# One core, a hybrid decoder block: the RWKV chunk chain with both heads in one matmul, the first two projection tiles in token halves, and the second up product added into the first one's copy

## The chip, the cores and the metric

The kernel is one program on one NeuronCore of a Trainium2 chip. The metric is the device time of one execution in microseconds (us); lower is better. Three runs of the kernel before took 2916.89 to 2919.65 us, with a median of 2918.94 us. TensorE (PE) multiplies; VectorE (DVE), ScalarE (ACT) and GpSimd (POOL) work on tiles; the queue of SyncE (SP) and the queues of ACT and POOL issue DMA transfers.

## The reference, cut to what matters

The block takes x of 512 tokens by 2048 channels in float32. It normalises x, projects it to 9,152 columns of several kinds, runs RWKV-7 time mixing (16 heads of 64) and sliding-window attention side by side, merges both with gates, projects back, and adds a gated ConvFFN of width 5632.

```python
h = rms_norm(x, norm1_g[l])
z = h @ w_in[l]                       # every projection; token shift on the RWKV part
def step(state, inp):                 # RWKV, for each head, token after token
    r_t, k_t, v_t, w_t, ka_t, kb_t = inp
    sa = jnp.einsum('bhvk,bhk->bhv', state, ka_t)
    state = (state * w_t[:, :, None, :] + sa[..., None] * kb_t[:, :, None, :]
             + v_t[..., None] * k_t[:, :, None, :])
    y = jnp.einsum('bhvk,bhk->bhv', state, r_t)
    return state, y
x = x + (g_rw * p_rw + g_att * p_att) @ w_out[l]
u = h2 @ w_up                         # h2 = rms_norm(x, norm2_g); then a causal conv of
val, gate = jnp.split(c, 2, axis=-1)  # width 3 over tokens gives c
x = x + (silu(gate) * val) @ w_down
```

## The kernel before, in words

**Precision.** A float32 operand of a large product is split into a high part (`whi`, `xhi`: an ACT copy to the type float32r) and the rest (`wlo`, `xlo`: a DVE subtraction), and three float32r matmuls replace one exact one: hi by hi, hi by lo, lo by hi. Small products stay plain float32; the trace shows each of those as two PE instructions.

**Order.** A planner orders the instructions of each engine by its own cost model and then every engine runs its list strictly in that order. `pin` (`tc.keep_in_program_order`) puts an instruction behind the one written just before it for the same engine, so the planner may not move it ahead; an instruction without `pin` may be moved ahead of earlier ones.

**Start (L291 to L310).** Four x tiles of 128 tokens are loaded and squared for the norm. In two halves of 256 tokens they are scaled (L297) and transposed on PE block by block (L304), and each block is evicted to `xhi` by ACT (L306) and to `xlo` by DVE (L307). Only when all 16 blocks of both halves exist does the first projection tile start.

**Projection tiles (`ztile`, `project`, `load_w`).** A tile is 128 columns of `w_in` for all 512 tokens: 16 blocks of 128 input channels by three matmuls of 512 columns (L259 to L261) into one PSUM bank. `load_w` (L241 to L245) loads four blocks of weights by SP into one of four `raw` buffers and splits them. After each third `load_w` it sends one job ahead for later stages (`sums_along`): SP copies half a megabyte in DRAM (L228) and POOL adds another half to it by DMA (L229). The first tiles are a key tile and a value tile of the attention (`c_ka`, `c_va`).

**RWKV (L464 to L800).** Heads go in eight pairs, one head in partitions 0 to 63 and one in 64 to 127. `early(p)` makes a pair's inputs with three projection tiles, `late(p)` builds and inverts the within-chunk matrices and then runs the chain over eight chunks of 64 tokens; `final(p)` and three gate tiles follow. While the chain of one pair waits, the planner fills PE with the next pair's projections and the gate tiles. In the chain each head has matmuls of its own, with 64 columns of weights and 64 moving columns, into its half of the partitions: `psG` (L744), `psS` (L755), and for the output `y` the products with `MM` (L765) and `BAR` (L767). `psU` (L748) already takes both heads at once.

**Up stage (L1049 to L1290).** One Strassen-like scheme gives for each block f of 128 columns seven products P1, P2, P7, P6, P5, Q4, P3 of 24 matmuls of 256 columns each (L1095). The first four blocks run P1, then P2, then P7 for all four while the right-hand factors t3, t1, t2, b22, t4 are still being made by DVE and split (`split_q`: ACT copy L1042, DVE subtraction L1043). For these four, P1 sits in one half of a PSUM bank (X) and P2 in the other half (Z). P1 is copied to `t1` (L1104); P2 stays in Z until the tiles `u` exist, and only then does `out("P2")` write `u = t1 + Z` (L1115). P6, P5 and P3 are accumulated onto P1 in X, and between them ACT copies X out to `u` (L1111). `run(i)` prepares step i + 2 (`prep`: the sum of two weight blocks L1071, then `whi` L1077 and `wlo` L1078), issues the matmuls of step i and then takes its result out.

Of the kernel before, what the change touches and what calls it, by code (L numbers as in the profile page):

```python
# [135 lines left out]
def block_kernel(ctx: ExitStack, tc: tile.TileContext, d: Dims, a: dict, out: bass.AP):  # L136
# [94 lines left out]
    wp = {"n": 0, "step": 3}  # L231
# [5 lines left out]
    def load_w(src):  # L237
# [4 lines left out]
        hi = wp["hl"].tile([P, 512], F32R, name="whi", tag="whi")[:, :n].rearrange("p (k c) -> p k c", c=ncol)  # L242
        lo = wp["hl"].tile([P, 512], F32R, name="wlo", tag="wlo")[:, :n].rearrange("p (k c) -> p k c", c=ncol)
        act.activation(hi, raw, AF.Copy)  # L244
        dve.tensor_tensor(lo, raw, hi.bitcast(F32), op=ALU.subtract)  # L245
        wp["n"] += 1
        if wp["n"] % wp["step"] == 0:
            sums_along()()
        return hi, lo

    def project(acc, src, xhi, xlo, pre=()):
        nk = src.shape[1]
        for k0 in range(0, nk, 4):
            n = min(4, nk - k0)
            whi, wlo = pre[k0 // 4] if k0 // 4 < len(pre) else load_w(src[:, k0 : k0 + n])
            for j in range(n):
                k = k0 + j
                first, last = k == 0, k == nk - 1
                pe.matmul(acc, whi[:, j], xhi[:, k], start=first, stop=False)  # L259
                pe.matmul(acc, whi[:, j], xlo[:, k], start=False, stop=False)  # L260
                pe.matmul(acc, wlo[:, j], xhi[:, k], start=False, stop=last)  # L261
# [3 lines left out]
    sync.dma_start(sinkb, a["attn_sinks"].rearrange("(o h) -> o h", o=1).to_broadcast([P, d.HQ]))  # L265
    sync.dma_start(cst, a["cst"][:, P:])
# [17 lines left out]
    if True:  # L284
# [3 lines left out]
        with tc.tile_pool(name="x0_ps", bufs=6, space=PSUM) as ps0:  # L288
            ssum = p0.tile([P, NT], F32, name="ssum")
            HT = NT // 2  # L290
            for h in range(2):  # L291
                for t in range(h * HT, (h + 1) * HT):
                    sq = p0.tile([P, d.D], F32, name="sqx", tag="sqx", bufs=1)
                    act.activation(sq, xt[t], AF.Square, accum_out=ssum[:, t : t + 1])
                r = rsqrt_small(p0, ssum[:, h * HT : (h + 1) * HT], 1.0 / d.D, RMS_EPS)
                for t in range(HT):
                    dve.tensor_scalar(xt[h * HT + t], xt[h * HT + t], r[:, t : t + 1], None, op0=ALU.mult)  # L297
            first = {d.c_ka: [load_w(zt[d.c_ka][:, k0 : k0 + 4]) for k0 in range(0, min(NK, 12), 4)]}
            for h in range(2):
                hs = slice(h * HT * P, (h + 1) * HT * P)  # L300
                for k in range(NK):
                    ps = ps0.tile([P, HT * P], F32, name="ps_x", tag="x")
                    for t in range(HT):
                        pe.transpose(ps[:, t * P : (t + 1) * P], xt[h * HT + t][:, k * P : (k + 1) * P], ident)  # L304
                    g = col("n1g", k)
                    act.activation(xhi[:, k, hs], ps, AF.Identity, scale=g)  # L306
                    dve.scalar_tensor_tensor(xlo[:, k, hs], ps, g, xhi[:, k, hs].bitcast(F32), op0=ALU.mult, op1=ALU.subtract)  # L307
        xin.close()
        act.activation(bor, K["bo"], AF.Copy)
        act.activation(cenr, K["cen"], AF.Copy)  # L310

        accp = pa.enter_context(tc.tile_pool(name="accA", bufs=3, space=PSUM, side="right", reuse_waits="tile"))

        def ztile(c0):
            acc = accp.tile([P, S], F32, name="acc", tag="acc")
            project(acc, zt[c0], xhi, xlo, first.pop(c0, ()))
            return acc
# [156 lines left out]
        with ExitStack() as pr:  # L474
# [141 lines left out]
            def late(p, st):  # L616
# [123 lines left out]

                for n in range(NCH):
                    ps = chn.tile([P, C], F32, name="psG", tag="chn")
                    for h, (lo, hi) in enumerate(HV):
                        pe.matmul(ps[lo:hi], AB[:, n, h], SV[:, n, h], start=True, stop=True)  # L744
                    G = wk.tile([P, C], F32, name="G", tag="G", bufs=2)
                    dve.tensor_copy(G, ps)
                    ps = chn.tile([P, C], F32, name="psU", tag="chn")
# [5 lines left out]
                    ps = chn.tile([P, C], F32, name="psS", tag="chn")  # L753
                    for h, (lo, hi) in enumerate(HV):
                        pe.matmul(ps[lo:hi], KK[:, n, h], UV[:, n, h], start=True, stop=True)  # L755
                    for h, (lo, hi) in enumerate(HV):
                        dve.scalar_tensor_tensor(SV[lo:hi, n + 1, h], SV[lo:hi, n, h], ee[lo:hi, n : n + 1], ps[lo:hi],
                                                 op0=ALU.mult, op1=ALU.add)


                ps = bulk()
                for n in range(NCH):
                    for h, (lo, hi) in enumerate(HV):
                        dst = r3(ps)[lo:hi, n]
                        pe.matmul(dst, UV[:, n, h], MM[:, n, h], start=True, stop=n == 0)  # L765
                        if n:
                            pe.matmul(dst, SV[:, n, h], BAR[:, n, h, 1], start=False, stop=True)  # L767
                yhl = wk.tile([P, 2, S], F32R, name="yhl", tag="rhl")
                split(yhl[:, 0], yhl[:, 1], ps)
# [270 lines left out]
    def split_q(n, q):  # L1040
        hi, lo = (halves(x) for x in bq[n])
        act.activation(hi, q, AF.Copy)  # L1042
        dve.tensor_tensor(lo, q, hi.bitcast(F32), op=ALU.subtract)  # L1043
# [7 lines left out]
    class Block:  # L1051
# [46 lines left out]
        def out(self, n):  # L1098
# [3 lines left out]
            if n == "P1" and self.f < NPRE:  # L1102
                self.t1 = up.tile([P, TH], F32, name="t1", tag="t1", bufs=NPRE)
                pin(act.activation(self.t1, X, AF.Copy))  # L1104
                return

# [7 lines left out]
            else:  # L1114
                pin(dve.tensor_tensor(u, self.t1 if n == "P2" and self.f < NPRE else u, ps, op=ALU.add))  # L1115
# [78 lines left out]
    def run(i):  # L1194
# [3 lines left out]
        if n != "P2" or f >= NPRE:  # L1198
            B[f].out(n)
# [9 lines left out]
    with tc.tile_pool(name="sqp", bufs=1, side="right", reuse_waits="tile") as sqp:  # L1209
# [3 lines left out]
        for i in range(len(PRODUCTS)):  # L1213
# [6 lines left out]
            for c in range(NB["o"]):  # L1220
                steps_of("o", i, acc[nm], c, hp)
                if last and c == NB["o"] - 4:
                    transposed(tps, 0, q11)
                    split_q("b11", q11)
                if last and c == NB["o"] - 3:
                    transposed(tps, 1, q21)
                    split_q("b21", q21)
# [27 lines left out]
    dve.tensor_tensor(q12, q22, q12, op=ALU.subtract)  # L1255
    split_q("t3", q12)
    tcx.close()
    x1q.close()
    run(5)
# [5 lines left out]
    dve.scalar_tensor_tensor(q11, q11, -1.0, q22, op0=ALU.mult, op1=ALU.subtract)  # L1265
# [5 lines left out]
    dve.scalar_tensor_tensor(q21, q11, -1.0, q21, op0=ALU.mult, op1=ALU.subtract)  # L1271
# [10 lines left out]
    for f in range(2):  # L1282
        B[f].out("P2")
    for i in range(3 * NPRE, len(steps)):
        run(i)
        if steps[i] in ((2, "P6"), (2, "Q4")):
            B[2 + (steps[i][1] == "Q4")].out("P2")
# [106 lines left out]
```

## Time and profile before

| | us |
|---|---|
| median of three runs | 2918.94 |
| the profiled execution, its own time | 2915.49 |
| its span, first to last instruction | 2913.7 |
| PE busy | 2868.1 |
| DVE busy | 1970.2 |
| ACT busy | 1333.6 |
| PE busy in the first 35 us | 14.48 |
| PE busy from 1576 to 1683 us (107 us, the opening of the up stage) | 94.54 |
| PE busy from 340 to 1180 us (840 us, the RWKV pairs) | 837.27 |

How to read it: times count from the first instruction of the profiled execution. A row of a timeline gives start, duration, engine, line, operation, output and inputs, shape, number of instructions merged, and in brackets how long the engine had been idle and what ended that. Matmuls overlap in the array, so durations of neighbours overlap too; what one costs is the distance from its start to the next start. `PEclk` is the share of the TensorE clock that was granted.

### The profile page before, as it was taken

How to read it: one execution, taken by the hardware profiler on the slowest of the kernel's cores; microseconds unless marked ns; L12 is line 12 of the kernel's file. 1: busy time of each engine (PE TensorE's matmuls, PEld its weight loads, DVE VectorE, ACT ScalarE, POOL GpSimd, SP SyncE). 2: the span in 40 equal slices, each digit the busy share in tenths (PEclk: the TensorE clock that was granted, in tenths of full speed). 3: DMA queues.
4: the chain of work that ended last, by engine and by line, in shares of the span. 5: the costliest groups of instructions: out<-in, count | busy, mean ns of one | idle time of the engine just before them, and what ended most of it. 6: DMA issues, size and time to landing. Idle time of an engine off the chain costs nothing.

```text
span 2913.7 us, 46929 instructions
## 1 busy us (share of the span) xinstructions
PE 2868.1 (98%) x18014; PEld 2441.3 (84%) x18014; DVE 1970.2 (68%) x3383; ACT 1333.6 (46%) x2251; POOL 219.3 (8%) x286
## 2 busy tenths in 40 slices
PE   7999999999999999999999899999999999999999
PEld 5777777777777777788888899999999999888887
DVE  4577666667767766354567777787777777665565
ACT  4345435435435434322356455545555455544444
POOL 0001000000000000111000010111111100000000
PEclk9999999999999999999999999999999999999999
DMA  7856756656656655878877788988889888877775
GB/s 210 217 146 166 184 142 168 156 145 163 159 149 149 167 148 139 266 222 239 293 251 226 208 227 231 242 233 231 221 235 238 237 227 234 312 242 240 259 255 188
DMA packets 225137, 609.29 MB, mean 209 GB/s; under 512 B 24768, under 2 KB 44944, under 8 KB 223888
## 3 DMA queue, kind: packets, MB, share of 16 engines
q1 hardware_dynamic: 157504, 434.84, 45.9%
q0 software_dynamic: 36064, 132.14, 23.9%
q10 hardware_dynamic: 31344, 39.31, 4.0%
q8 instruction: 141, 2.31, 0.3%
q14 instruction: 84, 0.69, 0.1%
HBM read 556.54 MB, written 174.43 MB: 251 GB/s over the span
## 4 chain that ended last, share of the span: by engine, by line
PE 94%; DVE 2%; ACT 1%; DMA 1%; issue 0%; SPq 0%; DVEq 0%; ACTq 0%
PE X L1095 17%; PE acc L259 11%; PE X L962 11%; PE acc L261 11%; PE acc L260 11%; PE Y L1095 9%; PE Y L962 8%; PE Z L1095 4%; PE bulk L737 1%; PE bulk L690 1%; PE psG L744 1%; PE bulk L646 1%; PE psS L755 1%; PE mi L464 1%; PE scp L431 1%; PE bulk L554 1%
## 5 line engine op out<-in xcount | busy, mean ns | idle before, releaser
L259 PE MATMUL acc<-xhi,whi 128*128 128x512 f32 x1152 | 473.1, 411 | 5.0 <-ACT whi L244 3.1
L261 PE MATMUL acc<-xhi,wlo 128*128 128x512 f32 x1152 | 469.2, 408 | 0.0
L260 PE MATMUL acc<-xlo,whi 128*128 128x512 f32 x1152 | 467.1, 405 | 0.0
L244 ACT ACTIVATE whi<-raw 128x512 fp32r<-128x512 f32 x352 | 220.3, 630 | 492.8 <-PE acc L260 376.6
L955 DVE TENSOR_TENSOR wlo<-raw,whi 128x1024 fp32r<-128x1024 f32 x210 | 257.0, 1224 | 204.9 <-ACT whi L954 203.4
L245 DVE TENSOR_TENSOR wlo<-raw,whi 128x512 fp32r<-128x512 f32 x352 | 240.2, 689 | 207.3 <-ACT whi L244 195.4
L954 ACT ACTIVATE whi<-raw 128x1024 fp32r<-128x1024 f32 x210 | 222.8, 1061 | 287.9 <-PE X L962 147.1
L1095 PE MATMUL X<-b,whi 128*128 128x256 f32 x1472 | 270.2, 284 | 2.2 <-DVE u L1115 0.9
L1095 PE MATMUL X<-t,whi 128*128 128x256 f32 x1408 | 260.2, 285 | 8.7 <-DVE u L1115 8.3
L1078 DVE TENSOR_TENSOR wlo<-raw,whi 128x1024 fp32r<-128x1024 f32 x176 | 215.0, 1222 | 77.4 <-ACT whi L1077 77.2
L259 PEld LDWEIGHTS acc<-xhi,whi 128*128 128x128 f32 x1152 | 217.5, 189 | 52.8 <-ACT whi L244 4.4
L261 PEld LDWEIGHTS acc<-xhi,wlo 128*128 128x128 f32 x1152 | 217.3, 189 | 48.2 <-issue 2.2
L1095 PE MATMUL Y<-t,whi 128*128 128x256 f32 x1408 | 257.5, 283 | 0.0
L260 PEld LDWEIGHTS acc<-xlo,whi 128*128 128x128 f32 x1152 | 217.7, 189 | 44.9 <-issue 3.3
L1077 ACT ACTIVATE whi<-a 128x1024 fp32r<-128x1024 f32 x132 | 139.4, 1056 | 213.8 <-DVE a L1071 211.2
L1095 PEld LDWEIGHTS X<-b,whi 128*128 128x128 f32 x1472 | 230.3, 193 | 3.0 <-issue 2.3
L1095 PEld LDWEIGHTS X<-t,whi 128*128 128x128 f32 x1408 | 222.0, 194 | 9.3 <-DVE u L1115 5.7
L1095 PEld LDWEIGHTS Y<-t,whi 128*128 128x128 f32 x1408 | 220.1, 192 | 0.0
L1095 PE MATMUL X<-b,wlo 128*128 128x256 f32 x736 | 208.9, 284 | 2.1 <-DVE wlo L1078 2.1
L1078 DVE TENSOR_TENSOR wlo<-a,whi 128x1024 fp32r<-128x1024 f32 x132 | 161.7, 1225 | 67.7 <-ACT whi L1077 67.0
L1095 PE MATMUL X<-t,wlo 128*128 128x256 f32 x704 | 200.5, 285 | 0.0
L1095 PE MATMUL Y<-t,wlo 128*128 128x256 f32 x704 | 199.3, 283 | 0.0
(345 smaller groups left out, 5877.7 us busy)
## 6 DMA issues: line engine op xcount, KB each, us to landing
raw<-in_w_up_dram SPq DMA_DIRECT2D x180, 512.0 KB
raw<-in_w_z_dram SPq DMA_DIRECT2D x288, 256.0 KB
s_dn<-in_w_dn_dram POOLq DMA_DIRECT2D x88, 512.0 KB, 6.7
raw<-in_w_up_dram POOLq DMA_DIRECT2D x88, 512.0 KB, 8.1
raw<-s_dn SPq DMA_DIRECT2D x88, 512.0 KB
raw<-in_w_dn_dram SPq DMA_DIRECT2D x66, 512.0 KB
a<-in_w_up_dram SPq DMA_DIRECT2D x48, 512.0 KB
s_dn<-in_w_dn_dram SPq DMA_DIRECT2D x44, 512.0 KB
```

Of the source, the lines that this page charges most:

```text
L244: act.activation(hi, raw, AF.Copy)
L245: dve.tensor_tensor(lo, raw, hi.bitcast(F32), op=ALU.subtract)
L259: pe.matmul(acc, whi[:, j], xhi[:, k], start=first, stop=False)
L260: pe.matmul(acc, whi[:, j], xlo[:, k], start=False, stop=False)
L261: pe.matmul(acc, wlo[:, j], xhi[:, k], start=False, stop=last)
L431: pe.matmul(scp[e][:, j, k0:], qn[j][hs, ts], kd[g][hs, n * P - BLK + k0 : (n + 1) * P], start=True, stop=True)
L954: act.activation(whi, wr, AF.Copy)
L955: dve.tensor_tensor(wlo, wr, whi.bitcast(F32), op=ALU.subtract)
L962: pe.matmul(dst, l[:, q, ts], r[:, es], start=fst and j == 0, stop=lst and j == 2, skip_group_check=True)
L1077: pin(act.activation(hi, t, AF.Copy))
L1078: pin(dve.tensor_tensor(lo, t, hi.bitcast(F32), op=ALU.subtract))
L1095: pin(pe.matmul(ps, l[:, k], r[:, k], start=start and k + i == 0, stop=last and i == 2, skip_group_check=True))
```

## The change

**Chain.** `psG` and `psS` become one matmul each for both heads (128 columns of weights, 128 moving columns); the blocks that mix two heads are computed too and never read. `G` is taken out by ACT for one head and DVE for the other. `y` is made by one `MM` and one `BAR` matmul for a chunk into two PSUM banks, one for four chunks, and split in eight quarter pieces in place of one whole.

```diff
                 for n in range(NCH):
-                    ps = chn.tile([P, C], F32, name="psG", tag="chn")
-                    for h, (lo, hi) in enumerate(HV):
-                        pe.matmul(ps[lo:hi], AB[:, n, h], SV[:, n, h], start=True, stop=True)
+                    ps = chn.tile([P, 2, C], F32, name="psG", tag="chn")
+                    pe.matmul(heads2(ps), heads2(AB[:, n]), heads2(SV[:, n]), start=True, stop=True)
                     G = wk.tile([P, C], F32, name="G", tag="G", bufs=2)
-                    dve.tensor_copy(G, ps)
+                    act.copy(G[0:C], ps[0:C, 0])
+                    dve.tensor_copy(G[C:P], ps[C:P, 1])
...
+                    pe.matmul(heads2(ps), heads2(KK[:, n]), heads2(UV[:, n]), start=True, stop=True)
                     for h, (lo, hi) in enumerate(HV):
-                        pe.matmul(ps[lo:hi], KK[:, n, h], UV[:, n, h], start=True, stop=True)
+                        dve.scalar_tensor_tensor(SV[lo:hi, n + 1, h], SV[lo:hi, n, h], ee[lo:hi, n : n + 1], ps[lo:hi, h],
+                                                 op0=ALU.mult, op1=ALU.add)
...
+                for g in range(2):
+                    ps = bulk().rearrange("p (n h c) -> p n h c", h=2, c=C)
+                    for j in range(HN):
+                        n = g * HN + j
+                        pe.matmul(heads2(ps[:, j]), heads2(UV[:, n]), heads2(MM[:, n]), start=True, stop=n == 0)
+                        if n:
+                            pe.matmul(ps[:, j], heads2(SV[:, n]), BAR[:, n, :, 1], start=False, stop=True)
                     for h, (lo, hi) in enumerate(HV):
-                        dst = r3(ps)[lo:hi, n]
-                        pe.matmul(dst, UV[:, n, h], MM[:, n, h], start=True, stop=n == 0)
-                        if n:
-                            pe.matmul(dst, SV[:, n, h], BAR[:, n, h, 1], start=False, stop=True)
-                split(yhl[:, 0], yhl[:, 1], ps)
+                        own = [r3(yhl[lo:hi, e])[:, g * HN : (g + 1) * HN] for e in range(2)]
+                        split(own[0], own[1], ps[lo:hi, :, h])
```

**Start.** The first two tiles (`heads`) run in halves of 256 tokens, with `half_mm` issuing three matmuls of 256 columns for a block. The first tile's first half follows the transposes of the first token half; the second tile's first half is laid between the transposes of the second token half; the two second halves come last. All of this is pinned. The weights of both tiles have eight pairs of buffers of their own beside the x tiles. The PSUM ring of the transposes goes from six to five, the two small constant loads go behind the first weights on SP, and the two DRAM jobs that these loads used to send are sent after the 31st and the 34th `load_w`.

```diff
-    wp = {"n": 0, "step": 3}
+    wp = {"n": 2 * NK // 4, "step": 3}
...
-        if wp["n"] % wp["step"] == 0:
+        if wp["n"] % wp["step"] == 0 or wp["n"] in (31, 34):
...
+            r = scales(0)
+            for t in range(HT):
+                scaled(0, t, r, dve)
+            ws = [[], []]
+            for k in range(NK):
+                columns(0, k)
+                if k == NK // 2 - 1:
+                    r = scales(1)
+                if k >= NK // 2 and k % 2:
+                    weights(0, 2 * (k - NK // 2 - 1))
+            for t in range(HT):
+                scaled(1, t, r, act if t else dve)
+            sync.dma_start(cst, a["cst"][:, P:])
...
+            for k in range(NK):
+                half_mm(0, 0, k)
+            for k in range(NK):
+                if k % 4 == 0:
+                    weights(1, k)
+                columns(1, k)
+                half_mm(1, 0, k)
+            for i in range(2):
                 for k in range(NK):
...
+                    half_mm(i, 1, k)
```

**Up stage.** For the first four blocks P2 is added to `t1` by DVE right after its matmuls; `placed` later copies `t1` to `u` on ACT. The splits and subtractions that make t3, t1, t2, b22 and t4 are now pinned where they are written, and the split of t3 moves ahead by one step.

```diff
+            if n == "P2" and self.f < NPRE:
+                pin(dve.tensor_tensor(self.t1, self.t1, Z, op=ALU.add))
+                return
...
+        def placed(self):
+
+            pin(act.activation(us[self.f % 2][:, 0, 2 : 2 + TH], self.t1, AF.Copy))
...
-    dve.tensor_tensor(q11, q11, q12, op=ALU.subtract)
+    pin(dve.tensor_tensor(q11, q11, q12, op=ALU.subtract))
     transposed(tps, 1, q22, dg)
     tpx.close()
+    pin(dve.tensor_tensor(q12, q22, q12, op=ALU.subtract))
     run(4)
-    dve.tensor_tensor(q12, q22, q12, op=ALU.subtract)
-    split_q("t3", q12)
+    run(5, lambda: split_q("t3", q12))
...
-    dve.scalar_tensor_tensor(q11, q11, -1.0, q22, op0=ALU.mult, op1=ALU.subtract)
+    pin(dve.scalar_tensor_tensor(q11, q11, -1.0, q22, op0=ALU.mult, op1=ALU.subtract))
     split_q("t2", q11)
...
     for f in range(2):
-        B[f].out("P2")
+        B[f].placed()
```

More of the change, by code (lines that the diff above doesn't have):

```diff
@@ new lines, in weights, with half_mm @@
+            def weights(i, k):
+                ws[i].append(load_w(zt[(d.c_ka, d.c_va)[i]][:, k : k + 4], p0, 2 * NK // 4, pin))
+            def half_mm(i, h, k):
+                hs = slice(h * HT * P, (h + 1) * HT * P)
+                whi, wlo = (w[:, k % 4] for w in ws[i][k // 4])
+                for j, (l, r) in enumerate(((whi, xhi), (whi, xlo), (wlo, xhi))):
+                    pin(pe.matmul(heads[i][:, hs], l, r[:, k, hs], start=h == 0 and k + j == 0,
+                                  stop=k == NK - 1 and j == 2, skip_group_check=True))
```

101 lines of the change are left out of this document (53 added, 48 removed).

## The prediction, made before the changed kernel was run

> **What bounds the kernel now.** I read the page first (busy time by engine), then a table of stretches, then PE's timeline wherever a stretch is not full.
>
> ```profile
> PE 2868.1 (98%) x18014; PEld 2441.3 (84%) x18014; DVE 1970.2 (68%) x3383; ACT 1333.6 (46%) x2251; POOL 219.3 (8%) x286
> L245 DVE TENSOR_TENSOR wlo<-raw,whi 128x512 fp32r<-128x512 f32 x352 | 240.2, 689 | 207.3 <-ACT whi L244 195.4
> ```
>
> ```profile
> 0.00:35.00 35.00, 14.48 (x65) 11.37 (x66) 23.26 (x71) 24.07 (x46) 2.02 (x6) 0.99 0.79 263
> 340.00:1180.00 840.00, 837.27 (x5520) 631.57 (x5519) 560.96 (x1359) 362.84 (x812) 54.09 (x68) 1.00 0.61 154
> ```
>
> The columns of the stretches are PE, PE's weight loads, DVE, ACT and POOL busy, granted clock, DMA share and GB/s. PE is busy for 98% of the span, and in the RWKV pairs for 837 of 840 us, with DVE at 561 and ACT at 363: there, time is what PE's instructions take, and a us less of them is a us less of the whole. The first 35 us are the opposite: PE is busy for 14.5.
>
> **The start.** PE's and DVE's timelines, the clock in one stretch, and a piece of the chain of waits:
>
> ```profile
> 14.82 4.83 PE L304 MATMUL ps_x<-ident,xi 128*128 128x128 f32 x20 [14.82 <-DVE xi L297]
> 34.67 0.79 PE L259 MATMUL acc<-xhi,whi 128*128 128x512 f32 x1 [1.91 <-DVE xlo L307]
> 49.05 1.05 PE L334 MATMUL mi<-cst,sqq 128*128 128x2 f32 x8
> 60.06 0.39 PE L259 MATMUL acc<-xhi,whi 128*128 128x512 f32 x1
> ```
>
> ```profile
> 24.74 9.87 DVE L307 SCALAR_TENSOR_TENSOR xlo<-ps_x,par,xhi 128x256 fp32r<-128x256 f32 x25
> ```
>
> ```profile
> 36.00:37.00 1.00, 1.00 (x4) 0.71 (x4) 0.00 (x0) 0.00 (x0) 0.00 (x0) 0.50 0.00 0
> ```
>
> ```profile
> 1679.42 2.88 PE Y L1095 x24
> ```
>
> The reader is to see that the transposes begin at 14.82 us, that the first tile waits for the last `xlo` and begins only at 34.67, at half clock (36 to 37 us: 0.50), and that the third tile begins at 60.06. Between 34.67 and 60.06 stand the two tiles and about 1.5 us of small head products (the L334 row and one group more), which are not late work of these tiles; without them the two tiles would be done at 58.5.
>
> After the change DVE still paces the first token half. One `xlo` costs 9.87 / 25 = 0.395 us. From the first eviction near 17 us come 16 of them (6.3), four weight subtractions of 0.69 (2.5 where they follow one another) and 1 us of tiny norm instructions: about 26.5. The last transposes need the `xlo` five before, so PE ends them near 23 and goes into the first tile's 48 matmuls. 24 matmuls of 256 columns take 2.88 us, so 48 take 5.8 at full clock; a part runs at half clock, and the last four blocks wait for their weights until 26.5. I take their end at 30. Then come 16 times two transposes (some 0.33 with the changes between kinds of product) and three matmuls (0.36): 11.0. Then 96 matmuls: 11.5. That ends at 52.5 to 53 in place of 58.5: **-5.5 us**. If half clock lasts throughout the first half, it is -3.5; with none, -7. What hides the rest: the constants that move behind the weights are needed only after this stretch; the two DRAM jobs move to near 110 to 120 us, and would cost something only if a `raw` load came late there, which I leave at 0 to 2.
>
> **The chain.** PE's timeline in one chunk of one pair:
>
> ```profile
> 512.51 0.39 PE L260 MATMUL acc<-xlo,whi 128*128 128x512 f32 x1
> 512.83 0.33 PE L755 MATMUL psS<-UV,KK 128*64 128x64 f32 x2
> 513.00 0.28 PE L765 MATMUL bulk<-MM,UV 128*64 128x64 f32 x2
> 513.11 0.28 PE L767 MATMUL bulk<-BAR,SV 128*64 128x64 f32 x2
> 513.32 0.50 PE L261 MATMUL acc<-xhi,wlo 128*128 128x512 f32 x1
> 513.66 0.39 PE L259 MATMUL acc<-xhi,whi 128*128 128x512 f32 x1
> 513.89 0.39 PE L260 MATMUL acc<-xlo,whi 128*128 128x512 f32 x1
> 514.21 0.33 PE L744 MATMUL psG<-SV,AB 128*64 128x64 f32 x2
> 514.47 0.51 PE L261 MATMUL acc<-xhi,wlo 128*128 128x512 f32 x1
> 514.90 0.33 PE L744 MATMUL psG<-SV,AB 128*64 128x64 f32 x2
> 515.16 0.50 PE L259 MATMUL acc<-xhi,whi 128*128 128x512 f32 x1
> 515.50 0.39 PE L260 MATMUL acc<-xlo,whi 128*128 128x512 f32 x1
> 515.73 0.39 PE L261 MATMUL acc<-xhi,wlo 128*128 128x512 f32 x1
> 515.96 0.33 PE L748 MATMUL psU<-G,BX 128*128 128x64 f32 x2
> 516.10 0.48 PE L259 MATMUL acc<-xhi,whi 128*128 128x512 f32 x1
> 516.42 0.40 PE L260 MATMUL acc<-xlo,whi 128*128 128x512 f32 x1
> ```
>
> What costs time is the distance between starts. A projection matmul in a row of its own kind takes 0.23 (513.66 to 513.89). From 513.89 to 515.50 there are three of them and both heads' `psG`: 1.61 - 0.70 = 0.91 us for `psG`. The pieces: each `psG` (two instructions) takes 0.26, and the projection matmul on each side of it takes 0.10 more than alone. From 512.51 to 513.66 there are two projection matmuls and one head's `psS`, `MM` and `BAR`: 1.15 - 0.46 = 0.69, or 1.37 for both heads. So such a chunk costs 0.91 + 1.37 = 2.28 us. `psU`, which already uses 128 columns of weights, shows no extra before it (515.73 to 515.96: 0.23) and goes on after 0.14.
>
> ```profile
> 505.65 0.34 PE L744 MATMUL psG<-SV,AB 128*64 128x64 f32 x4
> 505.91 0.50 PE L259 MATMUL acc<-xhi,whi 128*128 128x512 f32 x1
> 1158.65 0.33 PE L744 MATMUL psG<-SV,AB 128*64 128x64 f32 x2
> ```
>
> Not every chunk is so split. In the first row both heads' `psG` stand together (x4) and take 0.26, as much as one head: their halves run side by side. I count 72 `psG` rows with one head between 392 and 1159 us, of which the last is shown, so about 36 of 64 chunks are split, and about half for `psS` too.
>
> ```profile
> 1584.87 0.38 PE L1026 MATMUL ps_t<-dg,x 128*128 128x128 f32 x2
> ```
>
> Merged, each product is two instructions of 128 columns. The nearest row is a float32 product of that shape: 32 instructions in 3.49 us (1584.87 to the next start at 1588.36, of the step whose row ends there), 0.109 each. A chunk then costs 2 x 0.109 for `psG` and 6 x 0.109 for the rest: 0.87.
>
> The sum: split `psG` 36 x (0.91 - 0.22) = 25; together 28 x (0.26 + 0.2 - 0.22) = 7; split `psS` groups 27 x (1.37 - 0.65) = 19; those that stand together cost some 0.8 by the same reading, 29 x 0.15 = 4; the last chunks, without `psS`, some 3. That is 58, with no change of kind left to pay. If the 0.10 on each side belonged to the change between float32r and float32 rather than to 64 columns, about 128 groups would keep 0.2: 26 us less, 32. `psU` is nearer to the first; I take **-50 us**, and keep 32 and 58.
>
> What the merge adds lies beside PE: an ACT copy for each chunk, and six more small pieces for each `yhl`, some 2 us a pair on engines with 477 and 279 us free. Behind the ACT copy of `G` waits only `psU`, for which the planner puts projections first. The second PSUM bank for `y` is taken when the first is nearly read.
>
> **The opening of the up stage.** PE's waits, then DVE's and ACT's rows:
>
> ```profile
> 1625.43 0.77 PE L1095 MATMUL X<-t,whi 128*128 128x256 f32 x2 [2.76 <-DVE u L1115]
> 1630.39 0.50 PE L1095 MATMUL X<-t,whi 128*128 128x256 f32 x2 [0.47 <-ACT u L1111]
> 1659.18 0.80 PE L1095 MATMUL X<-t,whi 128*128 128x256 f32 x2 [5.51 <-DVE u L1115]
> 1601.11 2.28 DVE L1265 SCALAR_TENSOR_TENSOR x<-x,x 128x2048 f32<-128x2048 f32 x1
> 1608.92 2.28 DVE L1043 TENSOR_TENSOR t<-x,t 128x2048 fp32r<-128x2048 f32 x1
> 1622.66 2.29 DVE L1043 TENSOR_TENSOR t<-x,t 128x2048 fp32r<-128x2048 f32 x1 [0.58 <-ACT t L1042]
> 1624.87 0.75 DVE L1115 TENSOR_TENSOR u<-t,X 128x256 f32<-128x256 f32 x2
> 1601.22 1.92 ACT L1042 ACTIVATE t<-x 128x2048 fp32r<-128x2048 f32 x1 [1.41 <-DVE x L1255]
> 1626.87 1.06 ACT L1077 ACTIVATE whi<-a 128x1024 fp32r<-128x1024 f32 x1 [4.24 <-DVE a L1071]
> ```
>
> PE waits three times for a read of Z by DVE or what follows it (2.76, 0.47 and 5.51). The change takes the read away, but the first of these waits only moves. P5 of block 0 may start when ACT has copied P6 out of X; that copy stands on ACT behind `whi` of the next P6, which waits for a sum on DVE (1626.87, 4.24 idle), and the sum stands behind the rest of t4 (1622.66). Before, the planner had drawn the subtraction for t2 ahead (1601.11) and put other work between it and its split (1608.92), and DVE waited 0.58 for t4. Now both are pinned back to back: DVE waits the length of an ACT split (1.92) for t2 and again for t4, about 1.0 more between P6's sum and its `wlo`, and does four sums of some 0.37 (half of 1624.87). Each of these sums waits for its P2 on PE, and behind it stands the `wlo` of two steps later, which has a step of 2.88 to spare. Extra: 1.9 + 1.3 + 1.0 + 1.5 = 5.7, less about 1 that DVE idles now and would not. The rest of t4 ends near 1629.7 and not 1624.9; sum, `whi` and copy add 2.7, and P5 starts at 1632.4 and not 1630.39. PE, idle for some 9 us at one place, restarts at half clock, which costs 1.7 to 3.4. The third wait may shrink by 1.3. **+3.5 us**, from 0 to +6.
>
> [...]
>
> **Sum.** -5.5 - 50 + 3.5 = -52. Against the profiled execution's own 2915.49 that is 2863.5. The median of the runs is 3.45 above that execution, so I predict **2867 us** for the median.
>
> **Rivals.**
> 1. The change of kind stays to be paid: chain -32, sum -34, 2885. For it: the row after `psU` is also late by 0.09 (516.10 to 516.42: 0.32). Against it: none before `psU`.
> 2. Slower. The halves run side by side already, and one merged product streams twice the columns: 480 instructions of 0.109 in place of 480 pairs that cost 0.055 (513.00 to 513.11 holds two). That is +26 in the chain, sum +24, 2943. It decides if nearly all halves stand together as at 505.65 and the 0.10 stays. Against it: the 72 rows.
> 3. The pairs don't shrink, because the chain through DVE and ACT sets their length: -2, 2917. Against it: PE's 837 of 840.
> 4. The opening of the up stage loses its three waits as the edit says: -9 there, sum -64, 2854. For it: DVE's `u` ends two of them. Against it: the queue behind t4.
>
> [...]
>
> **Chances.** Forecast 0.60 (2855 to 2878); rival 1 0.17; rival 4 0.14; rival 3 0.05; rival 2 0.04. The range runs from 2853 (rival 4, the low end of the start) to 2893 (rival 1 with the upper ends of the start and the up stage). About 0.2% either way is what a measurement of this kernel can tell from no change. Faster: 0.60 + 0.17 + 0.14 = 0.91; rival 3 is the same, 0.05; slower 0.04.
>
> **What would show it.** RWKV pairs some 6 us shorter each (now 107.3), with two-instruction `psG` rows of 128x128 and 0.23 before them: the chain. If 0.33 stands before them, rival 1. The third tile near 54: the start; if at 60, DVE or the clock held it. P6 of block 0 ahead of 1625 and P5 not ahead of 1630, after the shift of what precedes: the up stage. Pairs as long as now, or PE idle within them, would make the prediction wrong.

## The result, and the profile after

The changed kernel takes 2951.28 us (median of four runs, 2943.66 to 2954.63) against 2917.91 us for the kernel before (2916.80 to 2919.65): ratio 1.011, 95% interval 1.0088 to 1.0133. It is 33 us slower where the forecast had it 51 us faster. The profiled execution of the changed kernel has a span of 2952.3 us, 38.6 more than before. One execution in all that follows stands far apart from the others of its kernel (4281.74 us, of the start without early jobs) and is left out of that kernel's ratio and range.

The page of the changed kernel, first its span and PE's row, then the stretch of the RWKV pairs from the table of stretches (columns: PE, PE's weight loads, DVE, ACT, POOL, granted clock, DMA share, GB/s):

```profile
span 2952.3 us, 46337 instructions
...
PE 2856.6 (97%) x17630; PEld 2453.2 (83%) x17630; DVE 1979.9 (67%) x3406; ACT 1353.1 (46%) x2344; POOL 219.1 (7%) x286
```

```profile
340.00:1180.00 840.00, 793.48 (x4885) 613.50 (x4884) 557.53 (x1337) 371.01 (x875) 53.29 (x67) 0.97 0.61 148
```

PE has 11.5 us less work in all and yet the span is longer. In the stretch that was full before (837.27 of 840 us) PE is now idle for 46.5 us, and the granted clock is 0.97 instead of 1.00. So the time was not lost in what PE's instructions take, on which the forecast's sum stood; it was lost in PE waiting.

Where along the span: the views of one line give the first and last start of its instructions ("first to last"). First the product that opens each pair and the first step of the up stage, before:

```profile
L646 PE MATMUL bulk<-BAR,BKK x128: 377/379/484, 338.8 to 1093.6; 128*128 128x256 f32 x128
L1095 PE MATMUL X<-b,whi x1472: 278/283/416, 1576.2 to 2488.6; 128*128 128x256 f32 x184
```

and in the changed kernel:

```profile
L691 PE MATMUL bulk<-BAR,BKK x128: 377/379/767, 343.9 to 1133.4; 128*128 128x256 f32 x128
L1145 PE MATMUL X<-b,whi x1472: 278/283/362, 1607.9 to 2526.3; 128*128 128x256 f32 x184
```

The first pair begins 5.1 us late (343.9 against 338.8), the up stage 31.7 us late (1607.9 against 1576.2), and its last step is 37.7 us late (2526.3 against 2488.6). So the start and the attention lost 5.1 us, the pairs and what follows them up to the up stage 26.6, the up stage 6.0, and the rest 0.9.

PE's waits of the changed kernel say on what (columns: line waiting, what it waited for, us in total, times, longest):

```profile
PE bulk L691 <- DVE MM L695: 23.0, 6, 5.0
PE bulk L656 <- DVE lw L654: 17.4, 7, 2.9
...
PE X L1145 <- ACT u L1164: 13.6, 2, 9.4
PE acc L326 <- ACT whi L244: 4.1, 2, 3.6
...
PE scp L476 <- DVE sc L482: 2.5, 1, 2.5
```

The first two are waits in the pairs, six and seven times in eight pairs: 40 us. The third is the up stage, the last two the start and the attention.

**How a pair loses its time.** The kernel before opens `y`'s only bank at chunk 0 and runs the next pair's head statistics (tile `lg`) right behind it (PE's timeline):

```profile
709.97 0.28 PE L765 MATMUL bulk<-MM,UV 128*64 128x64 f32 x2
...
710.30 1.05 PE L334 MATMUL bulk<-cst,lg 128*128 128x2 f32 x8
```

In the changed kernel, the first bank opens at 736.88, and the statistics stand behind the first products into the second bank, which come at chunk 4; in the pair before this one, what follows from that is seen at its end (PE's timeline):

```profile
658.52 1.10 PE L656 MATMUL bulk<-lw,cst 128*128 128x512 f32 x2 [2.49 <-DVE lw L654]
...
687.54 3.40 PE L691 MATMUL bulk<-BAR,BKK 128*128 128x256 f32 x8 [4.50 <-DVE MM L695]
...
736.88 0.39 PE L814 MATMUL bulk<-MM,UV 128*128 128x128 f32 x2
...
751.86 0.39 PE L814 MATMUL bulk<-MM,UV 128*128 128x128 f32 x2
...
752.30 0.95 PE L379 MATMUL bulk<-cst,lg 128*128 128x2 f32 x8
```

Their input was long there (ACT wrote `lg` at 709.9). They are 15.4 us behind the opening of `y` (752.30 - 736.88) where they were 0.3 us behind it (710.30 - 709.97). From them follow the norm, its round trip through DRAM (`rsT`, `rsd`, `rsb`), `kk`, and the rest of `early(p + 1)`; it no longer fits beside the chain. Behind the chain PE then waits for `lw` (2.49), `final(p)` gets its norm late, and DVE stands in its list at the row that takes that norm, with the next pair's masks `AB` and `MM` queued behind (DVE's timeline, changed kernel):

```profile
684.38 0.69 DVE L835 TENSOR_TENSOR yc<-yc,rsb 128x512 f32<-128x512 f32 x1 [6.31 <-DMA rsb<-rsd]
...
686.05 0.42 DVE L694 TENSOR_TENSOR AB<-bulk,cst 128x256 f32<-128x256 f32 x1
...
686.98 0.42 DVE L695 TENSOR_TENSOR MM<-bulk,cst 128x256 f32<-128x256 f32 x1
```

DVE idles for 6.31 us, and PE (L691 at 687.54) waits 4.50 for the banks that `AB` and `MM` empty. DVE waits at this row in the kernel before too (seven times in the stretch of the pairs, 22.5 us in all and 4.8 at most, against 35.4 and 6.8 now), but there PE's waits for `MM` come to 0.3 us in all.

### The profile page after: what moved, and what is told of

The parts are those of the page before. It is cut to its first block, busy times and chain, and to the rows that moved or that the text cites. A ratio compares the mean times of both kernels' runs of the same rounds, so it can differ in the third digit from the quotient of the medians.

```text
span 2952.3 us, 46337 instructions
## 1 busy us (share of the span) xinstructions
PE 2856.6 (97%) x17630; PEld 2453.2 (83%) x17630; DVE 1979.9 (67%) x3406; ACT 1353.1 (46%) x2344; POOL 219.1 (7%) x286
## 4 chain that ended last, share of the span: by engine, by line
PE 84%; DVE 6%; DMA 6%; ACT 2%; issue 2%; SPq 0%; ACTq 0%; DVEq 0%
PE X L1145 16%; PE X L1012 10%; PE acc L262 9%; PE acc L261 9%; PE acc L263 9%; PE Y L1012 8%; PE Y L1145 8%; PE Z L1145 4%; DMA rsb<-rsd 2%; DMA rsd<-rsT 2%; DMA raw<-in_w_z_dram 1%; DVE wlo L245 1%; PE bulk L735 1%; PE bulk L691 1%; PE bulk L782 1%
## 5 line engine op out<-in xcount | busy, mean ns | idle before, releaser
L261 PE MATMUL acc<-xhi,whi 128*128 128x512 f32 x1120 | 458.8, 410 | 1.0 <-ACT whi L244 1.0
L262 PE MATMUL acc<-xlo,whi 128*128 128x512 f32 x1120 | 457.4, 408 | 0.0
L263 PE MATMUL acc<-xhi,wlo 128*128 128x512 f32 x1120 | 455.7, 407 | 0.0
```

## The experiments

In all of them the kernel before ran on the same chip; its medians were 2914.6 to 2914.9 us. Ratios are against it.

**The three edits, each alone.** The diff of the change falls into three parts that share no line: the start, the chain, the up stage. A fourth kernel keeps the chain's part but computes `y` as before:

```diff
-                for g in range(2):
-                    ps = bulk().rearrange("p (n h c) -> p n h c", h=2, c=C)
...
+                ps = bulk()
+                for n in range(NCH):
+                    for h, (lo, hi) in enumerate(HV):
+                        dst = r3(ps)[lo:hi, n]
+                        pe.matmul(dst, UV[:, n, h], MM[:, n, h], start=True, stop=n == 0)
...
```

> The kernel before with the start's edits alone. In the changed kernel's trace the work at 340 us is 5.1 us late, all of it from a stall near 143 us. Theory J (the two DRAM jobs that the start moves to about 120 us fill the DMA engines, so the rows of a head norm come back late, and DVE and then PE wait for them): the stall is there without the other edits, third tile's work 0.4 us early at 60 to 130 us, pairs begin 5 us late, 2923 us. Rival (the stall comes from another edit, or from the way in which the whole kernel is ordered): no stall near 143 us, 2917 to 2918 us.

> The kernel before with the chain's edits alone. Theory R (the next pair's head statistics stand in PE's list behind the first product into the second bank of y, at chunk 4 instead of chunk 0, and everything after them is late) and rival S (the chain is shorter, so the next pair's way through DVE and its DRAM round trips shows, wherever the statistics stand) both expect what the changed kernel's pairs show: period near 113 us instead of 107.3, statistics some 16 us later in the chain, 27 us more in all, 2945 us (2938 to 2950).

> The kernel before with the up stage's edits alone. In the changed kernel's trace this stage is 6.0 us longer. The reading of it: P6's result waits on ACT behind a weight copy whose sum stands behind t4's split on DVE; P5 of block 0 starts 58 us after the stage's first step instead of 54.2; 2924 us (2922 to 2926). Rival (the late pairs or the late transfers before this stage made it longer): 2916 to 2919 us.

> The chain's edits alone, but y stays as before: one matmul for each head, one bank, one split. psG and psS stay merged. Theory R: y's only bank opens at chunk 0, the next pair's statistics stand there again, no wait of 3 and 5 us per pair is left, and the merge of psG and psS shows as a gain: some 3 to 4 us a pair, 2890 us (2883 to 2900). Rival S: the chain is about as short as in the changed kernel, so the waits for DVE stay, period 110 us or more, 2935 us or more.

| | us, median | ratio, 95% interval |
|---|---|---|
| start alone | 2913.39 | 0.9998 (0.9988 to 1.0008) |
| chain alone | 2943.85 | 1.0105 (1.0074 to 1.0135) |
| up stage alone | 2922.11 | 1.0021 (1.0011 to 1.0032) |
| chain, y in one bank | 2899.88 | 0.9948 (0.9933 to 0.9963) |

Against 2914.58 the three parts give -1.2, +29.3 and +7.5: 35.6 together, where the whole change gave 33.4 (2951.28 - 2917.91). Within the spread of these runs they add up, and the chain's part carries the loss. Its waits in the pairs (chain alone) are those of the whole change:

```profile
PE bulk L646 <- DVE MM L650: 20.7, 7, 5.0
PE bulk L611 <- DVE lw L609: 17.2, 7, 3.5
```

With `y` in one bank they are gone; in the same stretch of that kernel PE waits 1.0 us once and 0.2 once, and the statistics stand at chunk 0 (PE's timeline):

```profile
704.74 0.33 PE L768 MATMUL bulk<-MM,UV 128*64 128x64 f32 x2
705.00 0.61 PE L334 MATMUL bulk<-cst,lg 128*128 128x2 f32 x4
```

So the merge of `psG` and `psS` alone is a gain, 105.1 us a pair against 107.3, and theory S (a shorter chain shows the latency anyway) already looks wrong; the gain of 2.2 us a pair is less than the 3 to 4 that theory R had. The start alone came out neither as theory J nor quite as its rival had it; it is taken up below.

**Order or number of banks.** Two kernels run the same matmuls for `y` as the changed kernel. One deals the chunks to the two banks in turn, so that the second opens at chunk 1 and both stay taken; the other gives `y` a bank of its own, which its two halves use one after the other, and takes it from the chain's two:

```diff
+                pss = [bulk().rearrange("p (n h c) -> p n h c", h=2, c=C) for _ in range(2)]
+                for n in range(NCH):
+                    j, ps = n // 2, pss[n % 2]
```

```diff
-            chn = pr.enter_context(tc.tile_pool(name="chn_ps", bufs=2, space=PSUM, reuse_waits="tile"))
+            chn = pr.enter_context(tc.tile_pool(name="chn_ps", bufs=1, space=PSUM, reuse_waits="tile"))
+            yps = pr.enter_context(tc.tile_pool(name="y_ps", bufs=1, space=PSUM, reuse_waits="tile"))
...
-                    ps = bulk().rearrange("p (n h c) -> p n h c", h=2, c=C)
+                    ps = yps.tile([P, S], F32, name="yb", tag="yb").rearrange("p (n h c) -> p n h c", h=2, c=C)
```

> The chain's edits alone, but the two banks of y take the even and the odd chunks, so the second one opens at chunk 1 and both stay taken until the chain's end. The same matmuls as in the changed kernel. Theory R: the next pair's statistics stand behind chunk 1's first product, some 4 us into the chain instead of 16; most of the waits of 3 and 5 us per pair go, pairs of 104 to 107 us, 2895 us (2885 to 2912). Rival B (two of three banks held through the chain leave the next pair too few, whatever the order): pairs stay near 113 us, 2935 us or more.

> The chain's edits alone, but y has one bank of its own and the chain one bank in place of two (each of its products waits for the one before it anyway). The same matmuls as in the changed kernel. Theory R: the next pair's statistics wait for no bank of y, no wait of 3 and 5 us per pair is left, and what the merged products save shows in full. From the run with y in one bank (105.1 us a pair, 2.2 saved by psG and psS) and the chain of the changed kernel (24.2 us for seven chunks where the kernel before has 30.3, with 6 fewer projection matmuls of 0.23 in it) pairs of 102 to 104 us, 2885 us (2872 to 2895). Rival S (a shorter chain shows the next pair's latency anyway): waits for DVE of 3 us or more per pair stay, pairs of 105 us or more, 2898 us or more.

In turn: 2885.43 us, ratio 0.9902 (0.9885 to 0.9919). A bank of its own: 2878.28 us, ratio 0.9873 (0.9858 to 0.9888). PE's timeline, first of the kernel that deals in turn (chunk 0's product into `y` stands at 699.01, chunk 1's into the second bank at 703.44), then of the one with its own bank:

```profile
703.44 0.39 PE L768 MATMUL bulk<-MM,UV 128*128 128x128 f32 x2
...
703.89 0.95 PE L334 MATMUL bulk<-cst,lg 128*128 128x2 f32 x8
```

```profile
694.59 1.03 PE L334 MATMUL bulk<-cst,lg 128*128 128x2 f32 x8
...
698.55 0.39 PE L770 MATMUL yb<-MM,UV 128*128 128x128 f32 x2
...
706.30 0.39 PE L260 MATMUL acc<-xlo,whi 128*128 128x512 f32 x1
706.54 0.38 PE L759 MATMUL psS<-UV,KK 128*128 128x128 f32 x2
706.76 0.39 PE L770 MATMUL yb<-MM,UV 128*128 128x128 f32 x2
706.98 0.39 PE L772 MATMUL yb<-BAR,SV 128*128 128x128 f32 x2
707.12 0.48 PE L261 MATMUL acc<-xhi,wlo 128*128 128x512 f32 x1
707.44 0.39 PE L259 MATMUL acc<-xhi,whi 128*128 128x512 f32 x1
707.67 0.39 PE L260 MATMUL acc<-xlo,whi 128*128 128x512 f32 x1
707.90 0.38 PE L748 MATMUL psG<-SV,AB 128*128 128x128 f32 x2
708.04 0.48 PE L261 MATMUL acc<-xhi,wlo 128*128 128x512 f32 x1
708.36 0.39 PE L259 MATMUL acc<-xhi,whi 128*128 128x512 f32 x1
```

The statistics always stand right behind the first product into the last bank of `y` that comes from the shared three: chunk 0, 1 or 4; and ahead of the chain when `y` takes none of them. That is what banks granted in program order give: a tile that comes later in the program gets no bank before the earlier ones have theirs. Two of three banks held through the whole chain cost little against that: the kernel that deals in turn holds two, is 7 us slower than the one with a bank apart, and 58 us faster than the chain's part as it was (2943.85 - 2885.43). Rivals B and S fall. With its own bank the pairs show no wait of that kind, and the stretch of the pairs is full again (waits, then the stretch):

```profile
PE bulk L647 <- DVE bon L614: 0.9, 1, 0.9
```

```profile
338.00:1127.00 789.00, 785.79 (x4961) 608.49 (x4960) 563.55 (x1358) 378.35 (x889) 54.04 (x68) 1.00 0.64 160
```

**The same edit on the whole change.**

> The whole change, with one edit: y has one bank of its own, and the chain one bank in place of two. Theory R: the same 65 us that this edit is worth in the chain's edits alone (2943.9 to 2878.3), so 2951 - 65 = 2886 us (2878 to 2892): the order in which the banks are taken is then the whole reason why the change is slower than the kernel before. If other parts of the change interact with the pairs, 2895 us or more.

2881.97 us, ratio 0.9884 (0.987 to 0.9897): 69 us less than the changed kernel ran, as theory R had it (65; the two ratios give (1.0110 - 0.9884) x 2915 = 66). Where one tile's bank comes from turns the change from 1.1% slower to 1.2% faster.

**The up stage.** Of its edits only the early additions. (Of t3 the whole change moves the subtraction ahead by one step; the split goes behind the matmuls of step 5.)

```diff
-    pin(dve.tensor_tensor(q11, q11, q12, op=ALU.subtract))
+    dve.tensor_tensor(q11, q11, q12, op=ALU.subtract)
...
-    run(5, lambda: split_q("t3", q12))
+    split_q("t3", q12)
...
+    run(5)
```

> Of the up stage's edits only the early addition of the second product into the first's copy; the subtractions and splits of the right-hand factors stay free for the planner, and t3's split stays where it was. Theory Q (the loss of 6 us comes from t2's and t4's subtraction and split standing back to back on DVE, which makes P6's weights late): the wait of 9.4 us before P5 of block 0 falls to some 3 us, and the two waits of 2.8 and 5.5 us for DVE are gone, 2910 us (2906 to 2914). Rival (the additions themselves crowd DVE, or P6's result waits on ACT in any order): 2918 us or more.

2917.54 us, ratio 1.0007 (0.9998 to 1.0017). The up stage's edits alone lose 7.5 us and the additions alone about 3, a loss that can't be told from none. DVE's, ACT's and PE's timelines of the up stage's edits alone, then PE's row of the additions alone:

```profile
1629.26 2.29 DVE L1043 TENSOR_TENSOR t<-x,t 128x2048 fp32r<-128x2048 f32 x1 [1.98 <-ACT t L1042]
1631.47 1.22 DVE L1071 TENSOR_TENSOR a<-a,raw 128x1024 f32<-128x1024 f32 x1
```

```profile
1632.80 1.06 ACT L1077 ACTIVATE whi<-a 128x1024 fp32r<-128x1024 f32 x1 [2.96 <-DVE a L1071]
1633.76 0.37 ACT L1114 ACTIVATE u<-X 128x256 f32<-128x256 f32 x1
```

```profile
1634.18 0.80 PE L1095 MATMUL X<-t,whi 128*128 128x256 f32 x2 [9.37 <-ACT u L1114]
```

```profile
1631.26 0.79 PE L1095 MATMUL X<-t,whi 128*128 128x256 f32 x2 [5.64 <-ACT u L1114]
```

DVE waits 1.98 for t4's high part, then makes the rest, then P6's sum; ACT splits the sum and only then copies P6 out; P5 of block 0 starts at 1634.18 where the kernel before had it at 1630.39. Unpinned it starts at 1631.26. Theory Q has the direction, and the pins are the larger part; but it promised a gain of 5 and a wait of some 3 before P5, and there is no gain and a wait of 5.64, since the wait for P6's copy takes the place of the waits for DVE in either order.

**The start.** Its gain came and went from one execution to the next (2909.40 to 2921.39 us in ten runs). Two kernels moved the DRAM jobs:

```diff
-        if wp["n"] % wp["step"] == 0 or wp["n"] in (31, 34):
+        if wp["n"] % wp["step"] == 0 or wp["n"] in (43, 46):
```

```diff
-        if wp["n"] % wp["step"] == 0 or wp["n"] in (31, 34):
+        if wp["n"] % wp["step"] == 0 and wp["n"] > 15 or wp["n"] in (61, 64, 67, 70, 73):
```

> The start's edits alone, but the two DRAM jobs that the start postponed go with the 43rd and the 46th load of weights, near 190 us, where the DMA engines are a third busy, instead of the 31st and the 34th near 115 us, where they are over nine tenths busy. Theory J (the spread of the start's kernel, 2909.4 to 2921.4 us, comes from head-norm rows that are late between 115 and 145 us): most runs near 2909 to 2911, median 2910 us. Rival W (it comes from late weights near 40 us, at the start itself): the same spread as the start's edits alone, median 2913 us.

> The start's edits alone, but no DRAM job goes with the 9th, 12th and 15th load of weights (30 to 45 us) and none with the 31st and 34th; the five go with the 61st, 64th, 67th, 70th and 73rd load, between 270 and 320 us. Theory W (in runs where the start gains little, a load of weights near 40 us lands late because it shares the DMA engines with these jobs, PE then idles for some 4 us and restarts at half clock): nearly all runs at 2907 to 2911 us, median 2909 us, ratio 0.998. Rival (the weights land late without them): median 2913 to 2916 us and the same spread of 12 us.

Jobs later: 2915.03 us (2908.60 to 2924.53), ratio 1.0000 (0.9986 to 1.0015). No early jobs: 2916.07 us (2912.39 to 2921.74), ratio 1.0000 (0.9991 to 1.0009). Neither kept the gain, and both theories, which promised some 2910, fall. The first start of the product that opens the first pair, from the profiled execution of each kernel that has the new start, shows what the executions did (338.8 before): start alone 333.2, whole change with the other bank 334.1, no early jobs 335.0, start and chain together 337.4, whole change 343.9, jobs later 346.2. Two of the six lost 5 to 7 us at one place and as much again at a second. (The fourth is by the projection work done still 5.3 us early at 284 us and loses the rest beside the five jobs that it has there.) The first place is a load of weights that lands late at 43 us. ACT's timeline, of the kernel with jobs later and then of the start alone:

```profile
43.71 0.63 ACT L244 ACTIVATE whi<-raw 128x512 fp32r<-128x512 f32 x1 [5.08 <-DMA raw<-in_w_z_dram]
```

```profile
39.38 0.63 ACT L244 ACTIVATE whi<-raw 128x512 fp32r<-128x512 f32 x1 [0.67 <-DMA raw<-in_w_z_dram]
```

The load was sent at 35.91 in both executions, so it took 7.8 us in one and 3.5 in the other (in the changed kernel 7.0, from 36.20 to 43.17). It is not a load of the first two tiles: the split that waits for it stands between two evictions of the second token half (37.92 and 43.70 in the changed kernel) where the program pins none, so it is one of the third tile's that the planner drew ahead. ACT runs its list in order, so the transposes' evictions and the second tile's last weights stand behind it, and PE waits for those (4.4 us with jobs later, 3.6 in the changed kernel).

The second is the head norm of the attention: the rows below are SP's and DVE's and PE's timelines of the changed kernel. The two DRAM jobs that the start postponed go at 109.69 and 120.74, and the norm's rows (`rsd`) are sent at 126.58 and read back (`rsb`) only at 136.19, 9.6 us later; DVE waits 2.93 for them and PE 2.51.

```profile
109.69 0.51 SPq L228 DMA_DIRECT2D s_o<-in_w_o_dram  x1
...
120.74 0.61 SPq L228 DMA_DIRECT2D s_o<-in_w_o_dram  x1
...
126.58 0.29 SPq L386 DMA_DIRECT2D rsd<-rsT  x1
...
136.19 1.12 SPq L390 DMA_DIRECT2D rsb<-rsd  x2
```

```profile
145.04 0.69 DVE L408 TENSOR_TENSOR qn<-zq,rsb 128x512 f32<-128x512 f32 x1 [2.93 <-DMA rsb<-rsd]
```

```profile
146.19 1.13 PE L476 MATMUL scp<-kd,qn 64*128 64x256 f32 x4 [2.51 <-DVE sc L482]
```

In the kernel before, the same leg took 5.7 us (`rsd` at 126.94, `rsb` at 132.61). It took 7.1 (121.41 to 128.49) in the start alone, which has the same two jobs there, and 7.3 (127.72 to 134.98) with jobs later, which has none; in neither did DVE wait for it. The kernel with jobs later sends its two at 163.46 and 173.11, not near 190 us as was meant, and its profiled execution lost its second time at a later such round trip (`rsd` at 170.91; PE waits 2.3 us at the same line). So the losses fall beside the jobs, but the same jobs also cost nothing in one execution; that they are the reason for the spread isn't shown, and the kernel without the early jobs has most of it too. What makes the weights near 40 us late in one execution and not in the next stays open.

**The parts that help, together.** The chain with its own bank and the start without the early jobs, the up stage as before:

> The kernel before with the chain's edits, y in a bank of its own, and the start as in the run without the early jobs; the up stage as before. If the two gains add: 2878 - 5.5 = 2873 us (2868 to 2878). If the start's gain is lost to transfers: 2876 to 2884 us.

2880.99 us, ratio 0.9875 (0.986 to 0.989): the start adds nothing that can be measured. No kernel of the study is measurably faster than the simplest, the chain's part with a bank of its own for `y`: 2878.28 us, 1.3% under the kernel before.

## Why the prediction was wrong

**The step that failed** is the last sentence on the chain: "The second PSUM bank for `y` is taken when the first is nearly read." True as far as it goes (ACT reads the first bank from 748.36 on, the second opens at 751.86), but costed at nothing, with nobody named who waits behind it. The next pair's tiles come from the same three banks later in the program, so they wait for that opening, at chunk 4 in place of chunk 0. The order of the chunks alone is worth 58 us (2943.85 - 2885.43), and a bank apart 65.6 (2943.85 - 2878.28), more than the chain's whole gain. The base of the sum, "a us less of them is a us less of the whole", held only as long as PE's list stayed full. Rival 3, the chain through DVE and ACT as what sets the pairs' length (2917, at 0.05), came nearest in kind, but it had no price for longer pairs, and what made them longer was not the chain's own length: the work meant to lie beside it started late. "Pairs as long as now, or PE idle within them" was the right sign to look for: PE was idle for 46.5 us there.

**The chain's own gain** was right in kind and too large. With the bank apart the pairs went from 107.3 to 102.7 us and the up stage starts 38 us earlier (1538.0 against 1576.2), where the sum said 50 (32 to 58). A merged chunk costs about what was forecast: from 706.30 to 708.36 stand five projection matmuls and `psS`, `MM`, `BAR` and `psG`, 2.06 - 5 x 0.232 = 0.90 us, against 0.87. But 0.18 of it is no product: before the merged products stands 0.23, the sign named for the forecast, while behind them the next projection still goes on after 0.32 (707.12 to 707.44, 708.04 to 708.36). So 0.09 behind such a group remains (0.32 - 0.23), with the chain's products all at 128 columns; what causes it isn't shown.

Distances between starts, summed over one pair each (661.12 to 768.38 before, 648.42 to 751.12 with the bank apart), say where the gain fell short: `psG` 3.38 to 1.95, `MM` and `BAR` 4.52 to 2.91, `psS` 1.93 to 1.90, `psU` 1.25 to 1.73, the 288 projection matmuls 74.61 to 72.63; -4.6 in all, 37 for eight pairs. The sum had 58 before it was rounded down to 50. Three terms were mis-sized. The largest is the 0.10 on each side, which I gave wholly to the 64 columns (26 us): the projections gave back 8 x 1.98 = 16. The products themselves (32 us) gave 8 x 3.07 = 25. And `psU`, left out of the sum, costs 8 x 0.48 = 4 more. The first is what rival 1 was about, and the truth lies between it (32) and the forecast.

**Rival 2**, that the halves run side by side and the merge streams twice the columns, would have cost 26 in the chain. Its 2943 lies nearest to the measured 2951.28, by luck alone: with the bank apart the same merge is worth -36 (0.9873).

**The start** was forecast at -5.5. Three of six profiled executions show it or most of it at the first pair (333.2, 334.1 and 335.0 against 338.8), a fourth a part (337.4), and two lost more than all of it; the median of the runs shows no gain. Where it was lost, one term is the "0 to 2" for a late load near the moved DRAM jobs: the loss beside them was a head norm's round trip, some 5 us in the changed kernel, though that the jobs cause it isn't shown. The other I left out: the second tile's splits and evictions share ACT's list with the third tile's splits, and a load that is late for the third tile stops the second. In the kernel before, the loads sent at 19.73 to 21.83 were split from 41.80 on, so a late one had time; in the changed kernel ACT was free for the load sent at 36.20 from 38.9 on.

**The up stage** went as told, queue by queue: P6's copy on ACT behind `whi`, this behind the sum, this behind t4's rest. PE idles 9.4 us before P5 of block 0, as told, and the third wait shrinks by 1.3 (5.5 to 4.2), as told. P5 is 3.8 us late against its stage's start where I had 2.0, and the stage loses 6.0 in the profile, the upper end of 0 to 6. The 1.7 to 3.4 for the clock was my estimate, with no row beside it. In the kernel before, the granted clock is 0.50 for 3.41 us around the wait of 2.76 (1625.2 to 1628.6) and for 6.83 us around the wait of 5.51 (1655.9 to 1662.7). In the up stage alone it is 0.50 from 1629.32 to 1639.56, three stretches of 3.41 us where the kernel before has one: from 1634.18 to 1639.47 PE gets through eight groups of three matmuls, which at the 0.36 us of a group at full clock (1639.86 to 1640.57 holds two) would take 2.9 and not 5.3, so this place cost some 2.4. Rival 4, the three waits simply gone, is out.

## What to carry to other kernels

Before a ring of PSUM banks is asked for one more tile, list who takes a bank from it next in the program and when the new tile can first be written: where banks are granted in program order, as here, that moment is the earliest at which all the others can start. A full PE says nothing on how long the work beside it would need if the cover were thinner; follow the next iteration's chain of DVE, ACT and DRAM round trips from its first instruction. And a tile with a long life may be worth a bank of its own, taken from a ring whose tiles wait for each other anyway: here that was 7 us better than dealing in turn.

## What was not expected of the hardware

Most of the waits in the pairs cost more than their idle time. Three neighbouring stretches of the changed kernel, 3.41 us each (columns as above; the granted clock is the first of the last three numbers):

```profile
656.33:659.74 3.41, 1.22 (x4) 0.73 (x5) 3.29 (x7) 0.00 (x0) 0.00 (x0) 1.00 0.46 122
659.74:663.15 3.41, 3.41 (x10) 2.65 (x9) 2.53 (x4) 1.23 (x2) 0.00 (x0) 0.50 0.51 186
663.15:666.56 3.41, 3.41 (x21) 2.94 (x20) 2.17 (x7) 0.69 (x2) 0.81 (x1) 1.00 0.70 117
```

PE was busy for 1.22 us of the first and was still given half the clock for the whole of the second, in which it was never idle: 10 matmuls where the third has 21. A wait of 2.49 us thus cost 1.7 us more. Of the thirteen waits in the first two rows of PE's waits, eleven are followed by half clock, nine times for 3.41 us and twice for 6.83, and these stretches begin whole multiples of 3.41 us apart. The other two are the shortest, of 1.15 us, and one of 2.94 us in this stretch, behind which the full clock goes on:

```profile
1106.88:1110.29 3.41, 1.51 (x5) 0.98 (x6) 3.32 (x6) 0.00 (x0) 0.00 (x0) 1.00 0.56 126
```

Of the stretches with the full clock in the pairs of the changed kernel, the fullest that is followed by half clock has PE busy for 1.41 us (from 990.84), and the emptiest that is not is this one, with 1.51. The chain alone has the two closer together: 1.45 us (from 531.06) is followed by half clock, 1.46 (from 667.59) is not. The forecast counted half clock at the start and behind some 9 us of idle time, and none in the pairs; here a stretch in which PE was busy for a third of the time (1.22 of 3.41 us) was enough.

By way of an estimate, 44.4 us at half clock over the pairs cost 22 us (granted clock 0.97). With 43.8 us more of idle time (46.5 - 2.7) that makes 66; less the 26.6 by which the pairs got longer, 39 are left as the chain's hidden gain, and the run with the bank apart shows 38.
